# A hybrid encoder trunk on one core: a fourth PSUM tile for the attention heads, a shorter schedule for the modulation chunks, and priority for two last features instead of one

## The chip, the cores and the metric

The kernel runs on one core of one Trainium2 chip. Its time is the device time of one execution in microseconds (us). Three executions were timed before the change, and one more was profiled. TensorE (PE) does the matmuls, with its weight loads shown apart as PEld; VectorE (DVE), ScalarE (ACT) and GpSimd (POOL) work on vectors; SyncE (SP) issues the transfers.

## The reference

Two layers work on one sequence of 256 tokens with 2048 features, in float32:

```python
mod = c_act @ ada_w[l] + ada_b[l]                       # 6 x 2048 values: shift, scale, gate, twice
h = rmsnorm(x, norm_mix[l]) * (1.0 + sc_a) + sh_a
qa, ka, va, qb, kb, vb, ga, gb = split_cols(h @ w_in[l])
ya = window_attention(qa, ka, va, sink_a[l]) @ w_proj_a[l]      # 8 heads, 2 key heads, rotary
yb = neighbourhood_attention(qb, kb, vb, rel_bias_b[l]) @ w_proj_b[l]   # 8 heads
merged = jax.nn.sigmoid(ga) * ya + jax.nn.sigmoid(gb) * yb
x = x + gt_a * (merged @ w_out[l])
h = rmsnorm(x, norm_ffn[l]) * (1.0 + sc_m) + sh_m
u = depthwise_conv(h @ w_up[l], conv_w[l], conv_b[l])
g, v = jnp.split(u, 2, axis=-1)
x = x + gt_m * ((jax.nn.silu(g) * v) @ w_down[l])
```

rmsnorm divides by the root of the mean square of x, so each of the two norms of a layer needs the sum of the squares of all 2048 features, and the next product can be scaled only when the last feature of x is there.

## The kernel before

**Weights.** All matrices are streamed in the order of their use, 1 MB at a time: a unit is 16 blocks of 128x128. A unit is loaded into one of four `raw` buffers (L319). It is then halved into two parts `hl` of eight blocks: ACT casts the high part (L327) and DVE subtracts it from the original for the low part (L328). There are four `hl` buffers, so two units are held at a time. For a block PE multiplies the high weights with the high activations, and adds the two mixed products: three matmuls for most matrices (L374 to L376 with features of x in columns, L448 to L450 with tokens), and two for w_up and w_down where activations lie side by side (L370, L371). A name such as `hl_98_0` is the first half of unit 98, and `ps_98_16` the PSUM tile whose product begins behind unit 98's last block before it.

**Order of a layer.** Units 0 to 99 are w_in, w_proj_a, w_proj_b and w_out, units 100 to 231 w_up and w_down in three groups. During w_in of layer 0 the attention heads run on the side, one step of each live head per unit. A head's steps take PSUM tiles from the pool `ax`: `qtp` for the turned queries and keys (L681, evicted by ACT into packA or packB at L682), `sc` for the scores (L710), `tp` for the turned probabilities (L742), `po` for the result (L750). The projections themselves accumulate in the pool `mm` of four tiles.

**Squares' sums.** As each feature block `mo` of x (0 to 15) gets its residual (L1122), ACT squares it (L499) and DVE adds the square to `sqa` (L501); of the last block the square is kept apart. A matmul with a column of 1/2048 then sums `sqa` over the partitions (L508, `first`), and another the last square (`squares`). The tile for that (`ssm` behind w_out, `ssf` behind w_down) has a PSUM bank of its own, with a tag `ss`. The scaled features for the next product (`bare`, L596 and L597) are made at the same time, without the root, which is applied to the products later.

**Modulation.** The product for `mod` is done on DVE, in 192 chunks of 1 MB in each of which one column of 128 values is made (L227 loads, L230 multiplies and sums; all but three are loaded into the `raw` buffers too). The tables `ADA_PLAN_0` and `ADA_PLAN_1` say how many chunks are to be done when a unit of a layer is reached, with straight lines between the corners. The end of layer 0 needs 96 chunks for its own gates, and layer 1's first norm 32 of the next 96.

**Scheduler.** The tile framework puts the instructions of each engine into an order by their priority and readiness, so a short edit moves many instructions. In the code `urgent(...)` gives a block a higher priority than what comes before it in the program: the last features of w_out (both layers) and of the last w_down group are marked so, from `mo >= ENDING` on, and their units are fetched ahead (`prefetch`).

In w_out the features 13, 14 and 15 begin in the tiles ps_97_16, ps_98_16 and ps_99_16, each with 48 matmuls. In the last w_down group features 13, 14 and 15 are ps_230_9, ps_231_6 and ps_232_3, each with 26 matmuls.

Of the kernel before, what the change touches and what calls it, by code (L numbers as in the profile page):

```python
# [9 lines left out]
F32 = mybir.dt.float32  # L10
# [46 lines left out]
FIRST_TURN = 3  # L57
OUT_TURNS = [range(0, FIRST_TURN)] + [[mo] for mo in range(FIRST_TURN, KC)]

ADA_PLAN_0 = [(38, 32), (58, 48), (76, 66), (84, 70), (98, 80), (108, 80), (231, 132)]  # L60
ADA_PLAN_1 = [(8, 132), (76, 164), (84, 168), (99, 176), (108, 176), (128, 184), (142, 192)]

HASTE = range(76, 108)
FIRST_PLAN = [(0, 6), (10, 17), (42, 48)]

LEAD = 52
ENDING = 15

WARM_IN = [8, 4, 6]
WARM_ROW = 16  # L70
# [76 lines left out]
def encoder(ctx: ExitStack, tc: tile.TileContext, a: dict, out: bass.AP):  # L147
# [8 lines left out]
    at = pool("at", 2)  # L156
    sm = pool("sm", 3)
    mm = pool("mm", 4, space=bass.MemoryType.PSUM)
    ax = pool("ax", 3, space=bass.MemoryType.PSUM)

    ident = const.tile([P, P], F32, name="ident")
    make_identity(nc, ident[:])
# [327 lines left out]
    class Squares:  # L490


        def __init__(self, name):
            self.acc = ev.tile([P, S], F32, name="sqa", tag="sqa", bufs=1)
            self.ps = ax.tile([P, 2, 2], F32, name=name, tag="ss", bufs=1)

        def add(self, mo):
            sq = self.acc if mo == 0 else ev.tile([P, S], F32, name="sq", tag="z")
# [10 lines left out]
                )  # L509

        def first(self):
            self.total(0, self.acc)
            self.head = sm.tile([P, 2], F32, name="nsa", tag="nsa")
            nc.vector.tensor_scalar(out=self.head[:], in0=self.ps[:, 0], scalar1=EPS, scalar2=None, op0=ALU.add)

    def rsqrt(dst, src, n, k):

# [48 lines left out]
    class Bare:  # L566
# [36 lines left out]
        def squares(self):  # L603
            self.sums.total(1, self.sums.last)
            ss = sm.tile([P, 2], F32, name="nss", tag="nss")
            nc.vector.tensor_tensor(out=ss[:], in0=self.sums.head[:], in1=self.sums.ps[:, 1], op=ALU.add)  # L606
            self.rs = roots(ss)

        def roots(self):
# [199 lines left out]
    with tc.high_priority():  # L809
        one = place("b0", 12, F32, "one")[:1, 0, :P]  # L810
        nc.vector.memset(one, 1.0)
        cbs = []
        for i in range(0, D, 512):
            cbs.append(mm.tile([P, 512], F32, name="cb", tag="mm"))
            nc.tensor.matmul(cbs[-1][:], one, cact[:1, i : i + 512], start=True, stop=True)

        def activated(i):
            tc.keep_in_program_order(
                nc.scalar.activation(out=cact[:, 512 * i : 512 * (i + 1)], in_=cbs[i][:], func=AF.Silu)
            )  # L820

        sqs = []
        for i in range(KC // 4):
            sq = place(("y0", "y1", "y2", "a")[i], 12 if i == 3 else 4, F32, f"sq_in{i}")
            xs = x[:, 4 * i : 4 * i + 4]
            if i == 1:
                nc.vector.tensor_tensor(out=sq[:, :4], in0=xs, in1=xs, op=ALU.mult)
                activated(0)
                activated(1)
            else:  # L830
                tc.keep_in_program_order(nc.scalar.activation(out=sq[:, :4], in_=xs, func=AF.Square))
            sqs.append(sq)
        activated(2)
        activated(3)
        acc = sqs[0]
        for sq in sqs[1:]:
            nc.vector.tensor_tensor(out=acc[:], in0=acc[:], in1=sq[:, :4], op=ALU.add)
        nc.vector.tensor_tensor(out=acc[:, :2], in0=acc[:, :2], in1=acc[:, 2:4], op=ALU.add)
        warm(WARM_IN[0])
        ps = ax.tile([P, 2], F32, name="ss_in", tag="ss", bufs=1)  # L840
        for t in range(2):
            for i in range(2):
                tc.keep_in_program_order(
                    nc.tensor.matmul(
                        ps[:, t : t + 1], acc[:, i, t * P : (t + 1) * P], mean[:], start=i == 0, stop=i == 1
                    )
                )
        warm(WARM_IN[1])
        nc.scalar.activation(out=mean_sq[:], in_=ps[:], func=AF.Identity, bias=eps[:])

    tables = []

# [457 lines left out]
```

## Time and profile before

| | us |
|---|---|
| three executions | 2565.88, 2569.01, 2570.2 |
| median | 2569.01 |
| profiled execution | 2565.51 |
| its span on the core | 2563.7 |
| PE busy, DVE busy, ACT busy | 2538.5, 2205.4, 1451.8 |

A row of a timeline gives start, duration, engine, line, operation and tiles; brackets hold the idle time just before and the instruction that ended it. PE's matmuls are pipelined, so durations overlap; what counts is the distance between starts. The duration of a 256-column matmul is shown as 0.28 us, while starts are 0.11 us apart.

### The profile page before, as it was taken

The numbers are of one execution on the slowest core, as the hardware profiler recorded it, in microseconds if no ns is written. First come the engines' busy times: TensorE is split into PE (matmuls) and PEld (weight loads), VectorE is DVE, ScalarE is ACT, GpSimd is POOL, SyncE is SP. The second block draws the span as 40 slices with busy tenths as digits, with TensorE's granted clock in tenths as the row PEclk, the third lists the DMA queues.
The fourth block names the chain that finished last, engine by engine and source line by source line (L and its number), as shares of the span: only waits on it lengthen the run. The fifth ranks groups of instructions, "written<-read, shape, count | busy, mean of one in ns | idle before, by whom it ended". The sixth has DMA issues, their size and how long they took to land.

```text
span 2563.7 us, 39982 instructions
## 1 busy us (share of the span) xinstructions
PE 2538.5 (99%) x15636; PEld 2322.9 (91%) x15636; DVE 2205.4 (86%) x3159; ACT 1451.8 (57%) x2388; POOL 256.6 (10%) x329
## 2 busy tenths in 40 slices
PE   8999999999999999999999999999999999999999
PEld 7888888899999999999998888999999999999998
DVE  8999998998998899799987788979889987766775
ACT  5445865456664565456565676554576546654663
POOL 0000100000000000000004678720000000000000
PEclk9999999999999999999999999999999999999999
DMA  9998789886788778777767676777848875555554
GB/s 373 354 348 309 256 320 362 330 317 224 262 293 303 261 281 302 287 280 283 275 228 279 263 278 263 299 295 295 294 167 295 297 288 203 197 199 203 205 198 148
DMA packets 102143, 699.75 MB, mean 273 GB/s; under 512 B 12865, under 2 KB 15169, under 8 KB 18113
## 3 DMA queue, kind: packets, MB, share of 16 engines
q1 hardware_dynamic: 101954, 697.20, 73.4%
q8 instruction: 122, 2.00, 0.3%
q14 instruction: 67, 0.55, 0.1%
HBM read 695.06 MB, written 2.10 MB: 272 GB/s over the span
## 4 chain that ended last, share of the span: by engine, by line
PE 72%; DVE 15%; DMA 4%; issue 3%; ACT 3%; POOL 2%; SPq 0%; DVEq 0%; ACTq 0%; POOLq 0%
PE ps L370 31%; PE ps L371 16%; DVE hl L328 6%; PE ps_t L449 5%; PE ps_t L450 5%; PE ps_t L448 5%; DVE aw L230 4%; DMA aw<-in_aw 4%; PE ps L376 3%; PE ps L374 3%; PE ps L375 2%; ACT hl L327 1%; POOL packA L302 1%; DVE x L1122 1%; DMA w<-in_ws 1%
## 5 line engine op out<-in xcount | busy, mean ns | idle before, releaser
L328 DVE TENSOR_TENSOR hl<-w,hl 128x1024 fp32r<-128x1024 f32 x928 | 1131.0, 1227 | 232.0 <-ACT hl L327 229.4
L327 ACT CAST hl<-w 128x1024 fp32r<-128x1024 f32 x928 | 966.1, 1049 | 597.6 <-PE ps L371 263.0
L370 PE MATMUL ps<-h,hl 128*128 128x512 f32 x2432 | 796.8, 382 | 0.0
L371 PE MATMUL ps<-h,hl 128*128 128x256 f32 x2432 | 662.9, 273 | 0.0
L370 PEld LDWEIGHTS ps<-h,hl 128*128 128x128 f32 x2432 | 459.7, 189 | 63.9
L371 PEld LDWEIGHTS ps<-h,hl 128*128 128x128 f32 x2432 | 466.9, 192 | 0.0
L230 DVE CUSTOM_DVE_ANT_0 aw<-aw,cact,ab 128x2048 f32<-128x2048 f32 x189 | 444.5, 2353 | 9.9 <-DMA aw<-in_aw 9.8
L449 PE MATMUL ps_t<-hl,h 128*128 128x512 f32 x960 | 366.2, 382 | 4.1 <-DVE hl L328 3.8
L448 PE MATMUL ps_t<-hl,h 128*128 128x512 f32 x960 | 363.1, 383 | 3.8 <-ACT h L555 2.0
L450 PE MATMUL ps_t<-hl,h 128*128 128x512 f32 x960 | 364.7, 380 | 0.0
L449 PEld LDWEIGHTS ps_t<-hl,h 128*128 128x128 f32 x960 | 181.9, 190 | 34.1 <-DVE hl L328 9.1
L448 PEld LDWEIGHTS ps_t<-hl,h 128*128 128x128 f32 x960 | 181.1, 189 | 31.2 <-ACT hl L327 4.1
L450 PEld LDWEIGHTS ps_t<-hl,h 128*128 128x128 f32 x960 | 181.8, 189 | 25.7 <-DVE h L556 0.2
L370 PE MATMUL ps<-act_o,hl 128*128 128x512 f32 x512 | 170.5, 382 | 0.0
L1149 DVE SCALAR_TENSOR_TENSOR u<-both,cw,u 128x255 f32<-128x255 f32 x304 | 146.2, 481 | 3.8
L376 PE MATMUL ps<-merged,hl 128*128 128x256 f32 x512 | 140.9, 275 | 0.9 <-DVE hl L328 0.9
L374 PE MATMUL ps<-merged,hl 128*128 128x256 f32 x512 | 140.9, 276 | 0.4 <-DVE gb L481 0.4
L375 PE MATMUL ps<-merged,hl 128*128 128x256 f32 x512 | 140.7, 275 | 0.0
L371 PE MATMUL ps<-act_o,hl 128*128 128x256 f32 x512 | 139.6, 273 | 0.0
L1171 ACT COPY both<-ps 128x256 f32<-128x256 f32 x152 | 56.4, 371 | 124.6 <-PE ps L371 123.5
L1122 DVE SCALAR_TENSOR_TENSOR x<-ps,mod,x 128x256 f32<-128x256 f32 x224 | 105.6, 482 | 21.5 <-PE ps L371 19.4
L535 POOL TENSOR_TENSOR nrs<-nss,mhalf 128x2 f32<-128x2 f32 x3 | 2.1, 697 | 1173.6 <-DVE nss L606 1173.6
(264 smaller groups left out, 4336.4 us busy)
## 6 DMA issues: line engine op xcount, KB each, us to landing
w<-in_ws SPq DMA_DIRECT2D x463, 1024.0 KB, 4.8
aw<-in_aw SPq DMA_DIRECT2D x189, 1024.0 KB, 5.0
p<-in_bias SPq DMA_DIRECT2D x16, 256.0 KB, 3.6
x<-in_xT SPq DMA_DIRECT2D x4, 512.0 KB, 5.6
aw_o<-in_aw SPq DMA_DIRECT2D x2, 1024.0 KB, 12.4
out<-x SPq DMA_DIRECT2D x16, 128.0 KB, 1.8
w<-in_ws SPq DMA_DIRECT2D x2, 512.0 KB, 11.6
aw_b<-in_aw SPq DMA_DIRECT2D x1, 1024.0 KB, 16.8
```

The costliest lines, as they stand in the source:

```text
L230: product = nc.vector.tensor_tensor_reduce(out=raw[:], in0=raw[:], in1=cact[:], scale=1.0, scalar=ab[:, i : i + 1], op0=ALU.mult, op1=ALU. ...
L327: nc.scalar.copy(hl[:, 0], r)
L328: nc.vector.tensor_tensor(out=hl[:, 1], in0=r, in1=hl[:, 0].bitcast(F32), op=ALU.subtract)
L370: nc.tensor.matmul(ps[:], hi, act.both, start=first, stop=False)
L371: nc.tensor.matmul(ps[:, :S], lo, act.high, start=False, stop=last)
L374: nc.tensor.matmul(out, hi, act[0], start=first, stop=False)
L375: nc.tensor.matmul(ps[:, :S], hi, act[1], start=False, stop=False)
L376: nc.tensor.matmul(out, lo, act[0], start=False, stop=last)
L448: nc.tensor.matmul(ps[:], xh, hi, start=kc == kcs[0], stop=False)
L449: nc.tensor.matmul(ps[:], xh, lo, start=False, stop=False)
L450: nc.tensor.matmul(ps[:], xl, hi, start=False, stop=kc == kcs[-1])
L1149: nc.vector.scalar_tensor_tensor(out=u[:, to], in0=ps[:, of], scalar=w[:, j : j + 1], in1=u[:, to], op0=ALU.mult, op1=ALU.add)
```

## The change

It has three parts.

1. The pool `ax` has four PSUM tiles instead of three. The bank for it comes from the squares' sums, which no longer have one of their own: `first` takes a tile of `ax` when the sum is made, and `ss_in`, the same sum for the input, does so too.
2. The last corner of `ADA_PLAN_0` is at unit 216 instead of 231. The 52 chunks that were spread over units 108 to 231 now lie between 108 and 216, and there is none in the last 15 units of layer 0.
3. `ENDING` is 14 instead of 15. Features 14 and 15 have the priority, not feature 15 alone, in w_out of both layers and in the last w_down group of both layers.

```diff
-ADA_PLAN_0 = [(38, 32), (58, 48), (76, 66), (84, 70), (98, 80), (108, 80), (231, 132)]
+ADA_PLAN_0 = [(38, 32), (58, 48), (76, 66), (84, 70), (98, 80), (108, 80), (216, 132)]
...
-ENDING = 15
+ENDING = 14
...
-    ax = pool("ax", 3, space=bass.MemoryType.PSUM)
+    ax = pool("ax", 4, space=bass.MemoryType.PSUM)
...
         def __init__(self, name):
             self.acc = ev.tile([P, S], F32, name="sqa", tag="sqa", bufs=1)
-            self.ps = ax.tile([P, 2, 2], F32, name=name, tag="ss", bufs=1)
+            self.name = name
...
         def first(self):
+            self.ps = ax.tile([P, 2, S], F32, name=self.name, tag="ax")
             self.total(0, self.acc)
             self.head = sm.tile([P, 2], F32, name="nsa", tag="nsa")
-            nc.vector.tensor_scalar(out=self.head[:], in0=self.ps[:, 0], scalar1=EPS, scalar2=None, op0=ALU.add)
+            nc.vector.tensor_scalar(out=self.head[:], in0=self.ps[:, 0, :2], scalar1=EPS, scalar2=None, op0=ALU.add)
...
-            nc.vector.tensor_tensor(out=ss[:], in0=self.sums.head[:], in1=self.sums.ps[:, 1], op=ALU.add)
+            nc.vector.tensor_tensor(out=ss[:], in0=self.sums.head[:], in1=self.sums.ps[:, 1, :2], op=ALU.add)
...
-        ps = ax.tile([P, 2], F32, name="ss_in", tag="ss", bufs=1)
+        ps = ax.tile([P, 512], F32, name="ss_in", tag="ax")
...
-        nc.scalar.activation(out=mean_sq[:], in_=ps[:], func=AF.Identity, bias=eps[:])
+        nc.scalar.activation(out=mean_sq[:], in_=ps[:, :2], func=AF.Identity, bias=eps[:])
```

From line 512 on, the lines of the changed kernel have numbers that are higher by one.

The order on PE at the heads of layer 0, where unit 46 begins (a piece of the difference; - is before, + the change):

```order
-L681 MATMUL qtp<-ident,qn 128x128 x8
-L742 MATMUL tp<-ident,p 128x128 x4
+L682 MATMUL qtp<-ident,qn 128x128 x8
+L743 MATMUL tp<-ident,p 128x128 x4
+L711 MATMUL sc<-packA_209 128x256 x2
 L448 MATMUL ps_46_t_2200<-hl_46_0_2166,h_0_157 128x512
 L449 MATMUL ps_46_t_2200<-hl_46_0_2166,h_0_157 128x512
 L450 MATMUL ps_46_t_2200<-hl_46_0_2166,h_0_157 128x512
 L448 MATMUL ps_46_t_2201<-hl_46_0_2166,h_0_157 128x512
-L710 MATMUL sc<-packA_209 128x256 x2
```

The scores are put four matmuls earlier; around units 47 to 52 sc and tp move ahead by three to nine rows in the same way.

The order on PE in w_out of layer 0, before, where feature 13 (ps_97_16) ends:

```order
L375 MATMUL ps_97_16_0_5229<-merged_3993,hl_97_1_5235 128x256
L376 MATMUL ps_97_16_0_5229<-merged_3993,hl_97_1_5235 128x256
L374 MATMUL ps_98_16_0_5298<-merged_3993,hl_98_0_5301 128x256
L374 MATMUL ps_99_16_0_5379<-merged_3993,hl_99_0_5365 128x256
L375 MATMUL ps_99_16_0_5379<-merged_3993,hl_99_0_5365 128x256
L376 MATMUL ps_99_16_0_5379<-merged_3993,hl_99_0_5365 128x256
```

And in the change, where feature 12 (ps_96_16) ends:

```order
L376 MATMUL ps_96_16_0_5160<-merged_3993,hl_96_1_5166 128x256
L374 MATMUL ps_97_16_0_5228<-merged_3993,hl_97_0_5231 128x256
L374 MATMUL ps_98_16_0_5297<-merged_3993,hl_98_0_5300 128x256
L375 MATMUL ps_98_16_0_5297<-merged_3993,hl_98_0_5300 128x256
L376 MATMUL ps_98_16_0_5297<-merged_3993,hl_98_0_5300 128x256
L374 MATMUL ps_98_16_0_5297<-merged_3993,hl_98_0_5300 128x256
```

Before, feature 13 is finished first, and 14 stops after one matmul to let 15 pass. Now 13 stops after one matmul, 14 and 15 are done, and 13 comes last.

The order on DVE at the end of layer 0, before, from the residual of the feature that ends last (ps_231_6, feature 14) to the reading of its sum:

```order
L1122 SCALAR_TENSOR_TENSOR x<-ps_231_6_0_12205,mod_158,x 128x256
L328 TENSOR_TENSOR hl_1_0_12262<-w_1_12260,hl_1_0_12262 128x1024
L1122 SCALAR_TENSOR_TENSOR x<-ps_231_6_0_12205,mod_158,x 128x256
L328 TENSOR_TENSOR hl_1_1_12265<-w_1_12260,hl_1_1_12265 128x1024
L501 TENSOR_TENSOR sqa<-sqa,sq 128x256
L597 SCALAR_TENSOR_TENSOR bare_0_b_11589<-x,amod_8113,bare_0_b_11589 128x256
L514 TENSOR_SCALAR nsa<-ssf_11586 128x2
```

And in the change, where it is feature 13 (ps_230_9):

```order
L1123 SCALAR_TENSOR_TENSOR x<-ps_230_9_0_12163,mod_158,x 128x256
L602 TENSOR_TENSOR bare_0_qn<-mod_7859,bare_0_qn 128x1
L328 TENSOR_TENSOR hl_1_1_12264<-w_1_12259,hl_1_1_12264 128x1024
L1123 SCALAR_TENSOR_TENSOR x<-ps_230_9_0_12163,mod_158,x 128x256
L501 TENSOR_TENSOR sqa<-sqa,sq 128x256 x2
L598 SCALAR_TENSOR_TENSOR bare_0_b_11607<-x,amod_7864,bare_0_b_11607 128x256
L515 TENSOR_SCALAR nsa<-ssf_12288 128x2
```

One split instead of two stands between the residual's start and the sum, and two additions follow each other. On PE the first matmul of ssf comes 40 matmuls after the last one of w_down, where it came 31 after it.

## The prediction

> **What bounds the kernel now.** I read the page first, then who waited for whom on TensorE, then the stretches around each wait, then the order of time there. Two rows of the page, and the rows of PE's waits that belong to the places of the change (total us, times, longest):
>
> ```profile
> PE 2538.5 (99%) x15636; PEld 2322.9 (91%) x15636; DVE 2205.4 (86%) x3159; ACT 1451.8 (57%) x2388; POOL 256.6 (10%) x329
> L328 DVE TENSOR_TENSOR hl<-w,hl 128x1024 fp32r<-128x1024 f32 x928 | 1131.0, 1227 | 232.0 <-ACT hl L327 229.4
> ...
> PE ps_t L449 <- DVE hl L328: 3.8, 10, 0.6
> PE ps L376 <- DVE hl L328: 3.4, 5, 1.5
> PE sc L710 <- ACT packB L682: 2.4, 1, 2.4
> PE ssf L508 <- DVE sqa L501: 1.5, 1, 1.5
> PE tp L742 <- ACT packB L682: 0.7, 2, 0.4
> ```
>
> TensorE is busy for 99% of the 2563.7 us, so the change can win only where it waits, or where its clock is lowered. Of the waits above, sc and tp (3.1 us) are for a PSUM tile of the heads, ssf (1.5 us) is for the sum of squares, and the rest is for weights: `hl` is the halved weight that ACT casts (L327) and DVE completes (L328). Behind the two longest waits the granted clock falls. The columns are the stretch, its length, busy us of PE, PEld, DVE, ACT and POOL, the granted clock and the DMA:
>
> ```profile
> 276.00:279.00 3.00, 1.00 (x6) 0.54 (x4) 3.00 (x5) 2.97 (x13) 0.00 (x0) 1.00 0.82 309
> 279.00:283.00 4.00, 3.56 (x9) 2.90 (x10) 3.84 (x10) 3.63 (x13) 0.00 (x0) 0.57 0.56 188
> 283.00:292.00 9.00, 9.00 (x51) 7.83 (x51) 8.02 (x18) 7.91 (x29) 1.64 (x1) 1.00 0.79 292
> 292.00:331.00 39.00, 38.26 (x215) 33.89 (x213) 38.39 (x89) 35.09 (x95) 5.24 (x2) 1.00 0.59 210
> 331.00:386.00 55.00, 55.00 (x275) 48.67 (x274) 54.97 (x83) 31.73 (x59) 0.00 (x0) 1.00 0.90 340
> 386.00:440.00 54.00, 54.00 (x267) 47.72 (x266) 47.63 (x64) 29.04 (x47) 0.00 (x0) 1.00 0.97 362
> ...
> 1306.00:1311.00 5.00, 5.00 (x32) 5.00 (x32) 1.46 (x3) 0.84 (x2) 0.70 (x1) 0.66 0.67 231
> ...
> 1628.00:1636.00 8.00, 6.49 (x58) 6.30 (x57) 8.00 (x12) 3.96 (x6) 5.64 (x7) 1.00 0.73 265
> ```
>
> So one lowered spell costs 4 us x (1 - 0.57) = 1.7 us, and 5 us x (1 - 0.66) = 1.7 us the other time. It followed a wait of 2.4 us and one of 1.5 us; the 1.5 us wait for weights around 1630 (the longest of L376) was not followed by one.
>
> **The heads of layer 0 (fourth tile).** What can be removed on TensorE is 2.4 (sc) + 1.7 (spell) + 0.7 (tp) = 4.8 us. With four tiles sc and tp no longer stand behind the eviction of qtp (packB, L682), so I take these waits as gone. But how much reaches the end is decided by the weights. DVE has no room: from 276 to 331 us it is idle for 55 - (3.00 + 3.84 + 8.02 + 38.39) = 1.75 us, from 331 to 386 for 0.03 us, and its order there is almost the same in the changed kernel. The halves just ahead of that, as DVE finishes and as PE takes them:
>
> ```profile
> 328.14 1.22 DVE L328 TENSOR_TENSOR hl<-w,hl 128x1024 fp32r<-128x1024 f32 x1
> 331.37 0.38 PE L449 MATMUL ps_t<-hl,oA 128*128 128x512 f32 x1
> ...
> 336.03 2.35 DVE L328 TENSOR_TENSOR hl<-w,hl 128x1024 fp32r<-128x1024 f32 x2
> 337.43 0.38 PE L449 MATMUL ps_t<-hl,oA 128*128 128x512 f32 x1
> ```
>
> The first is ready at 329.36 and used 2.0 us later; the first of the two at 336.03 is ready at about 337.25 and used 0.18 us later. A TensorE that is 4.8 us early waits there for all but 0.2 us of it, unless DVE is early too. DVE can be early by no more than its idle 1.75 us. More than half of that is one wait in the heads' own chain, behind sc and the exponentials:
>
> ```profile
> 286.45 0.16 DVE L726 TENSOR_TENSOR den<-den,es 128x2 f32<-128x2 f32 x1 [0.98 <-ACT es L725]
> ```
>
> That one goes, and a part of the rest: I take 1.2 us as won. After 386 us the transfers run at 0.97, and PE waits for weights again around 454 to 474 us (the row of 440 to 480 us):
>
> ```profile
> PE ps_t L449 <- DVE hl L328: 1.3, 3, 0.6
> ```
>
> There everything is tied to transfers, which start earlier by what DVE is early. **-1.2 us**; bounds 0 (DVE wins nothing) and -4.8 (all is kept).
>
> **Priority for feature 14, w_out of layer 0.** The two last features are now both ahead of feature 13, so unit 98's weights are asked for 48 matmuls earlier, before feature 13's own:
>
> ```profile
> 586.95 0.28 PE L374 MATMUL ps<-merged,hl 128*128 128x256 f32 x1
> 592.20 0.28 PE L376 MATMUL ps<-merged,hl 128*128 128x256 f32 x1
> 592.97 0.38 PE L376 MATMUL ps<-merged,hl 128*128 128x256 f32 x1 [0.16 <-DVE hl L328]
> 603.46 0.28 PE L374 MATMUL ps<-bare_a,hl 128*128 128x258 f32 x1
> ...
> 587.16 1.98 ACT L327 CAST hl<-w 128x1024 fp32r<-128x1024 f32 x2
> 588.25 1.23 DVE L328 TENSOR_TENSOR hl<-w,hl 128x1024 fp32r<-128x1024 f32 x1
> ```
>
> The first two rows are 47 matmuls apart, 0.1115 us each. At 586.95 PE starts feature 13 with one matmul and then wants unit 98 at 587.07. Its first half is cast by 588.20 (the two casts at 587.16 overlap; the first takes 1.03) and completed by DVE at 589.48. The high half costs 588.20 - 587.07 = 1.1 us of waiting, two matmuls follow, and the low half costs 589.48 - 588.46 = 1.0 us. Then both halves of unit 97 stay held, so both halves of unit 99 go through the one buffer that unit 98's first half frees at about 592.0; cast 1.03 and split 1.22 make it ready at 594.3 against a use at 594.2, and the second is as tight: 0.2 us together. Before, the same 144 matmuls took 603.46 - 586.95 = 16.51 us for 144 x 0.1115 = 16.06, so 0.45 is given back. 1.1 + 1.0 + 0.2 - 0.45 = **+2.0 us** (rounded up by the hand-over of some 0.04 us at each wait); bounds 0, if the scheduler's order lets the splits come earlier, and +3.7, with a spell of lowered clock behind it. The two waits have matmuls between them and neither reaches 1.5 us, so I count no spell.
>
> **The same in layer 1.**
>
> ```profile
> 1845.46 0.28 PE L374 MATMUL ps<-merged,hl 128*128 128x256 f32 x1
> 1862.86 0.28 PE L374 MATMUL ps<-bare_a,hl 128*128 128x258 f32 x1
> ...
> 1843.49 2.35 DVE L230 CUSTOM_DVE_ANT_0 aw<-aw,cact,ab 128x2048 f32<-128x2048 f32 x1 [0.96 <-DMA aw<-in_aw]
> 1846.50 2.36 DVE L328 TENSOR_TENSOR hl<-w,hl 128x1024 fp32r<-128x1024 f32 x2
> ```
>
> Here a modulation chunk (L230, 2.35 us) stands on DVE ahead of the split of unit 98's first half, the second of the two at 1846.50, which ends at 1848.86. After one matmul on unit 97, the two high ones on unit 98 and three more, PE is at 1846.13: a wait of 2.75 us; later 0.2 as above. Before, 17.40 us for 16.06 of matmuls: 1.35 given back. 2.75 + 0.2 - 1.35 = +1.6. This wait is longer than both that were followed by a spell, so I add one: 1.6 + 1.7 = **+3.3 us**; bounds 0 and +4.3, if the chunk, which itself waited 0.96 us for its transfer, lands 1 us later.
>
> [...]
>
> **w_down at the end of layer 0 (no chunks, priority).**
>
> ```profile
> 1287.54 0.38 PE L370 MATMUL ps<-act_o,hl 128*128 128x512 f32 x1
> 1303.83 0.28 PE L374 MATMUL ps<-bare_a,hl 128*128 128x258 f32 x1
> 1305.64 0.61 PE L508 MATMUL ssf<-mean,sqa 128*128 128x1 f32 x4 [1.53 <-DVE sqa L501]
> ...
> 1284.25 2.37 DVE L230 CUSTOM_DVE_ANT_0 aw<-aw,cact,ab 128x2048 f32<-128x2048 f32 x1
> 1288.45 1.24 DVE L328 TENSOR_TENSOR hl<-w,hl 128x1024 fp32r<-128x1024 f32 x1
> 1303.64 0.48 DVE L1122 SCALAR_TENSOR_TENSOR x<-ps,mod,x 128x256 f32<-128x256 f32 x1
> 1305.16 0.42 DVE L501 TENSOR_TENSOR sqa<-sqa,sq 128x256 f32<-128x256 f32 x1
> ```
>
> ssf costs 1305.64 - 1303.94 = 1.7 us, the spell 1.7, some 0.1 besides: 3.5 us. Now ssf has 40 matmuls ahead of it since the last group's end instead of 31 (0.1115 each: 1.0 us later), and feature 14's square is added long before; only 13's residual (L1122, twice, with one split between), square and two additions follow the last matmul: about 0.5 + 1.2 + 0.5 + 0.4 + 0.7 = 3.3 us plus a wait for the cast of 0.6, against 4.5 us of matmuls. So ssf does not wait. Against it: unit 231's first half is now wanted 13 matmuls after 1287.54 (0.164 us each, a long and a short one being 0.33), at 1289.7. DVE, without the chunk of 1284.25, comes to its end after three splits (1.13 us from start to start), four residuals and a modulated copy (0.39 each) and an addition (0.34): 5.7 us, at 1290.0. With the cast and small hand-overs I take 0.7 us of waits. -3.5 + 0.8 = **-2.7 us** (0.1 for what else comes late); bounds -3.5 and 0.
>
> **The chunks' new place.** Seven chunks more between units 108 and 216, 7 x 2.35 = 16.5 us of DVE:
>
> ```profile
> 650.00:1210.00 560.00, 560.00 (x3484) 516.67 (x3483) 502.67 (x711) 316.06 (x470) 0.00 (x0) 1.00 0.77 285
> ```
>
> DVE goes from 502.67 to 519 of 560 us (93%), PE does not wait there in this row, and the transfers are at 0.77. **0**; bounds 0 and +1.5, where a half comes late by part of one chunk. If the cover went, it would cost at most those 16.5 us.
>
> **The kernel's end.** The last group's features end in the other order; after the last matmul the same two residuals remain:
>
> ```profile
> 2559.92 1.00 DVE L1122 SCALAR_TENSOR_TENSOR x<-ps,mod,x 128x256 f32<-128x256 f32 x2 [3.04 <-PE ps L371]
> ```
>
> A wait for unit 231's weights as at the end of layer 0, less hidden work: **+0.3 us** (0 to +0.5). Layer 1's heads hardly change their order, and their waits there are for hl: 0. The squares' sums in the other pool take a tile for three instructions at the seams, when no head runs: 0.
>
> **Sum.** -1.2 + 2.0 + 3.3 - 2.7 + 0 + 0.3 = +1.7 us. The profiled execution took 2565.51 us; the median is 3.5 above it, so on the median's basis I say 2569.0 + 1.7 = **2570.7 us**: no change, since 0.2% (5.1 us) is about what a measurement of this kernel can tell.
>
> **Rivals.** (A) The weights follow: the first splits after the heads come early enough, or transfers do, and the 4.8 us stay; the earlier splits of units 98 and 231 hide the new waits. -4.8 - 2.7 = -7.5: 2561.5. For it: 2.0 us of slack at 331. Against: 0.18 us at 337 and a full DVE. (B) Slower: the waits for unit 98 take the place of those removed, and lowered clock follows all of them, at w_out in both layers and at w_down, where the wait for unit 231 grows past 1.5 us and eats the gain. -1.2 + 3.7 + 3.3 + 0 + 0.3 = +6.1: 2575.1. It decides from 1.5 us of waiting in one piece; for it speaks 1306, against it 1630. (C) No spell follows in either layer, as around 1630: +1.7 - 1.7 = 0.0: 2569.0. [...] (D) The fourth tile does not help, because sc waits for packB's data and not for the tile: then -1.2 goes, and 2572. Against it: sc reads packA, and packB is only what frees the tile.
>
> **Chances.** Forecast 0.38, C 0.17, D 0.08, A 0.14, B 0.23. A is the faster case, with 0.02 from C's lower edge: 0.16. B is the slower one: 0.23. Same: 0.61. The forecast's own range is 2567 to 2573; to hold 8 in 10 it reaches to A's upper part and past B: 2563 to 2576.5.
>
> **What would show it.** Right: no sc or tp among PE's waits, clock 1.00 from 276 to 283; new waits of ps_t for hl between 331 and 345 us and longer ones at 454 to 474; ps L374 or L376 waiting about 2 us near 588 and 2.8 near 1846; no wait of ssf, clock 1.00 from 1303 to 1312; DVE's busy share up from 650 to 1210. Wrong: PE passing 345 us more than 2 us earlier than before (then A), lowered clock at 588 or 1295 (then B), or a PE wait of over 1 us between 650 and 1210.

## The result and the profile after

| | before | after |
|---|---|---|
| median of 9 executions, us | 2568.71 | 2574.11 |
| lowest and highest, us | 2564.28, 2570.39 | 2571.7, 2580.4 |
| span of the profiled execution, us | 2563.7 | 2571.9 |
| ratio, with 95% interval | | 1.0037 [1.0027, 1.0047] |

The changed kernel is slower: by 5.4 us between the medians, 8.2 between the two profiled executions, and some 9.5 by the ratio, whose interval goes from 7 to 12 us. The forecast was 2570.7 us and no change. The time lies inside the wide range that was given (2563 to 2576.5) but above the forecast's own (2567 to 2573), and the direction was not the likeliest one: the slower case had a chance of 0.23.

On the page of the changed kernel, TensorE's row:

```profile
PE 2541.8 (99%) x15636; PEld 2324.1 (90%) x15636; DVE 2203.0 (86%) x3159; ACT 1448.5 (56%) x2388; POOL 259.4 (10%) x329
```

Its waits (total us, times, longest), those that belong to the places of the change:

```profile
PE ps L376 <- DVE hl L328: 4.5, 6, 1.5
...
PE po L751 <- ACT pT L465: 2.2, 1, 2.2
PE ps L371 <- DVE hl L328: 2.2, 5, 1.0
PE ps L374 <- ACT hl L327: 2.1, 3, 1.7
PE ssf L508 <- DVE sqa L501: 0.5, 1, 0.5
...
PE sc L711 <- ACT packB L683: 0.3, 1, 0.3
```

The waits for sc (2.4), tp (0.7) and most of the wait for ssf (1.5) are gone, as intended by the edits. New are `po`, a wait of 2.2 us in the heads; L371, five waits in w_up, where before there was none; and in the row of L374 one of 1.7 us for the first half of unit 98 in w_out (before, that row had 0.4 us in all). The stretches around them, with the columns as in the prediction (length, busy us of PE, PEld, DVE, ACT and POOL, granted clock, DMA):

```profile
285.00:290.00 5.00, 2.80 (x17) 2.27 (x16) 5.00 (x15) 4.88 (x19) 1.64 (x1) 0.96 0.92 375
290.00:293.00 3.00, 3.00 (x10) 2.46 (x9) 2.63 (x8) 2.76 (x12) 1.51 (x1) 0.50 0.37 93
...
587.00:592.00 5.00, 2.55 (x12) 2.25 (x12) 5.00 (x9) 3.48 (x6) 0.00 (x0) 0.80 0.99 375
592.00:597.00 5.00, 4.94 (x36) 4.68 (x36) 1.55 (x3) 1.14 (x2) 0.00 (x0) 0.86 0.81 284
...
1178.00:1228.00 50.00, 48.07 (x289) 43.22 (x288) 43.46 (x63) 28.84 (x46) 0.00 (x0) 1.00 0.74 274
...
1300.00:1320.00 20.00, 19.36 (x145) 18.23 (x145) 13.26 (x21) 10.10 (x15) 0.69 (x1) 1.00 0.48 158
```

To see where time goes for good, the same matmul of PE is looked up in two traces: the first one on a given unit. The table gives how much later (or, with a minus, earlier) it starts than in the kernel before. A step between two columns is what that stretch costs. It is worked out from the starts of PE's matmuls, one profiled execution of each kernel; e1 to e12 are the kernels of the experiments below. At 269 us alone the starts lie between 0.3 us earlier and 3.1 later, with the same edits or not, so steps count and not levels. One piece of the scatter has a size. Where the granted clock falls, it is at 0.50 for 3.4 us (before: 279.2 to 282.6 and 1306.6 to 1310.0 us; changed kernel: 289.6 to 293.0), in e5 from 1854 us on for twice that, which costs 1.7 us (or 3.4). The profiled execution of the kernel before has two such spells inside the table, from 279 and from 1307 us, so a kernel that does not have them steps by -1.7 there with no merit of its own.

| us before | 269 | 297 | 471 | 576 | 610 | 1096 | 1232 | 1316 | 1731 | 1840 | 1875 | 2539 |
|---|---|---|---|---|---|---|---|---|---|---|---|---|
| layer, unit | 0, 45 | 0, 48 | 0, 76 | 0, 95 | 0, 101 | 0, 193 | 0, 219 | 1, 2 | 1, 76 | 1, 96 | 1, 102 | 1, 228 |
| after | 0.2 | 0.5 | -0.7 | -0.1 | 5.0 | 5.0 | 8.6 | 6.5 | 6.3 | 6.9 | 7.7 | 7.7 |
| e1 | 1.7 | 2.0 | 1.5 | 3.1 | 3.3 | 3.3 | 3.3 | 1.6 | 1.5 | 2.5 | 2.4 | 2.4 |
| e2 | 1.8 | 0.4 | 0.5 | 1.2 | 1.4 | 1.4 | 4.8 | 1.5 | 1.8 | 2.5 | 1.2 | 1.2 |
| e3 | 1.8 | 0.4 | -1.0 | 1.0 | 5.7 | 5.7 | 5.7 | 4.6 | 4.9 | 10.4 | 15.4 | 15.4 |
| e4 | -0.3 | -1.7 | -2.7 | -2.8 | -3.2 | -3.2 | 0.2 | -3.1 | -3.4 | -3.2 | -1.9 | -1.9 |
| e5 | 2.3 | 2.8 | 2.1 | 2.4 | 5.5 | 5.4 | 8.9 | 5.6 | 5.5 | 5.6 | 11.2 | 11.2 |
| e6 | 1.7 | 2.5 | 2.3 | 2.3 | 1.9 | 1.9 | 5.9 | 3.7 | 3.5 | 4.6 | 4.0 | 4.0 |
| e7 | 3.1 | 3.4 | 2.2 | 2.1 | 2.3 | 2.3 | 2.3 | -1.0 | -1.3 | 1.9 | 1.9 | 1.8 |
| e8 | -0.1 | -1.4 | -2.6 | -2.6 | -3.0 | -1.8 | -1.8 | -5.1 | -5.4 | -4.4 | -5.6 | -5.6 |
| e9 | 1.9 | 2.0 | 7.8 | 21.6 | 21.2 | 21.2 | 21.2 | 19.5 | 19.7 | 20.4 | 20.2 | 20.2 |
| e10 | 1.5 | 1.7 | 10.0 | 25.3 | 25.9 | 25.9 | 25.9 | 24.6 | 24.4 | 28.7 | 33.1 | 33.1 |
| e11 | 1.7 | 2.1 | 1.3 | 1.3 | 0.9 | 0.9 | 0.9 | -2.4 | -2.6 | -1.3 | 1.4 | 1.4 |
| e12 | 1.6 | -0.7 | -0.8 | -0.5 | 0.1 | 0.1 | 0.1 | -1.5 | 1.5 | 2.7 | 3.2 | 3.2 |

For the changed kernel: two places cost, w_out of layer 0 (576 to 610 us: +5.1) and the chunks' new place (1096 to 1232: +3.7); the end of layer 0 steps by -2.2 and the heads, taken from 269 to 471, by -0.9. How much of these two the change has earned is a question for the experiments. The rest is small: 0.6 ahead of w_out, 1.4 around w_out of layer 1, and 0.5 behind the last column.

### The profile page after: what moved, and what is told of

Same layout as the page of the kernel before. It is cut to its first block, busy times and chain, and to the rows that moved or that the text cites. A ratio compares the mean times of both kernels' runs of the same rounds, so it can differ in the third digit from the quotient of the medians.

```text
span 2571.9 us, 39995 instructions
## 1 busy us (share of the span) xinstructions
PE 2541.8 (99%) x15636; PEld 2324.1 (90%) x15636; DVE 2203.0 (86%) x3159; ACT 1448.5 (56%) x2388; POOL 259.4 (10%) x329
## 4 chain that ended last, share of the span: by engine, by line
PE 72%; DVE 15%; ACT 4%; DMA 4%; issue 3%; POOL 2%; SPq 0%; ACTq 0%; DVEq 0%; POOLq 0%
PE ps L370 30%; PE ps L371 15%; DVE hl L328 6%; PE ps_t L449 5%; PE ps_t L450 5%; PE ps_t L448 5%; PE ps L376 4%; PE ps L374 4%; DVE aw L230 4%; PE ps L375 4%; ACT hl L327 2%; DMA aw<-in_aw 2%; DMA w<-in_ws 1%; POOL p L302 1%; POOL packA L302 1%
## 5 line engine op out<-in xcount | busy, mean ns | idle before, releaser
L371 PE MATMUL ps<-h,hl 128*128 128x256 f32 x2432 | 663.8, 273 | 2.2 <-DVE hl L328 2.2
L371 PEld LDWEIGHTS ps<-h,hl 128*128 128x128 f32 x2432 | 467.4, 192 | 3.9 <-DVE hl L328 3.9
L1150 DVE SCALAR_TENSOR_TENSOR u<-both,cw,u 128x255 f32<-128x255 f32 x304 | 146.0, 480 | 3.3
L374 PE MATMUL ps<-merged,hl 128*128 128x256 f32 x512 | 142.1, 278 | 2.1 <-ACT hl L327 1.7
L371 PE MATMUL ps<-act_o,hl 128*128 128x256 f32 x512 | 139.3, 273 | 0.0
L1123 DVE SCALAR_TENSOR_TENSOR x<-ps,mod,x 128x256 f32<-128x256 f32 x224 | 105.0, 480 | 36.0 <-PE ps L371 25.9
```

The costliest lines, as they stand in the source:

```text
L371: nc.tensor.matmul(ps[:, :S], lo, act.high, start=False, stop=last)
L374: nc.tensor.matmul(out, hi, act[0], start=first, stop=False)
L1150: nc.vector.scalar_tensor_tensor(out=u[:, to], in0=ps[:, of], scalar=w[:, j : j + 1], in1=u[:, to], op0=ALU.mult, op1=ALU.add)
```

## The experiments

The change has three parts, so the first three kernels do one each.

**e1, the fourth tile alone.**

```diff
 (the changed kernel with)
-(108, 80), (216, 132)]
+(108, 80), (231, 132)]
-ENDING = 14
+ENDING = 15
```

> Only the fourth tile (the squares' sums in the same pool); plan and priority as before. Theory M (read from the two traces): the wait of sc is gone, but one of about 2.2 us for ACT's pT takes its place some 7 us later, followed by a spell of lowered clock as before; what stays by 470 us is -1, and the whole is -1.1 to 0 us. Theory F (as forecast): -1.2 us, with the new waits being for hl between 331 and 345 us. If the heads' waits were worth what they show, -4.8 us.

Measured: 2566.16 us against 2567.54, ratio 0.9996 [0.9985, 1.0006]. From 269 to 471 us it wins 0.2 of the 4.8 us that stood on PE. The steps from 269 to 297 us show why. With the fourth tile they are +0.3 to +0.8 where a lowered clock follows the wait for po (after, e1, e5, e6, e7, e11) and -1.4 and -1.3 where none does (e4, e8). Without it they are 0 to +0.2 where a lowered clock follows the wait for sc (before, e9, e10) and -1.4 where none does (e2, e3). So the tile moved the wait to the next step of the heads and took nothing off it; what differs is the spell. From 269 to 471 us the kernels without the tile step by -1.3 (e2) and -2.8 (e3), so no gain of the tile can be told from the scatter there either.

**e2, the plan alone.**

```diff
 (the kernel before with)
-(108, 80), (231, 132)]
+(108, 80), (216, 132)]
```

> Only the plan: no chunk in the last 15 units of layer 0. Theory M: about +3 us from waits of PE for hl in units 209 to 217 (1180 to 1230 us), one each second unit, and the wait of ssf near 1304 stays within 0.5 us of its 1.7, since it hangs on the last feature and not on the chunks: +2 to +3.5. Theory F: 0 (DVE has room), -0.5 to +1.5.

Measured: 2566.87, ratio 0.9996 [0.9987, 1.0005]. Two steps cancel in the table: +3.4 from 1096 to 1232 us and -3.2 from 1232 to 1316. So the plan alone takes away the wait for ssf, which the prediction had credited to plan and priority together, and pays for it earlier; each of the two expectations had missed one of the steps. Half of the 3.2 us is not the plan's. e1, e9 and e12 have the old plan and the old order, and they wait for ssf for 1.5 us as the kernel before does, but their steps are -1.6 and -1.7, the cost of one spell that the kernel before has there and they, by these steps, do not. The lowered clock at 1307 belongs to that one execution of the kernel before. Against these three kernels the plan is worth some 1.6 us here, and it costs 3.4 in w_up.

**e3, the priority alone.**

```diff
 (the kernel before with)
-ENDING = 15
+ENDING = 14
```

> Only the priority for feature 14. Theory M: +5 us at w_out of layer 0 (about 1.8 and 1.0 us of waits near 587 us and a spell of lowered clock), +1 in layer 1, and at the end of w_down of layer 0 between -2.3 us (the order alone does it) and 0 (the chunks there spoil it): +3.5 to +6. Theory F: +2.0, +3.3, -2.7 and +0.3: +2.9.

Measured: 2574.77, ratio 1.0031 [1.002, 1.0041]. This part is slower alone: +4.7 at w_out of layer 0, and +5.0 at w_out of layer 1 (1840 to 1875; 5.5 more came from 1731 to 1840, where e7 without the priority also loses 3.3). At the end of layer 0 its step is -1.1, smaller than that of e1, e9 and e12, which have neither plan nor priority: there the priority alone costs half a microsecond.

**e4, tile and plan, without the priority.**

```diff
 (the changed kernel with)
-ENDING = 14
+ENDING = 15
```

> The fourth tile and the plan, priority as before: the sum of the first two if they do not touch each other. Theory M: +1 to +3.5. Theory F: -1.2. If the parts are separate, this and the third kernel add up to the whole change (+5.4 us).

Measured: 2567.25, ratio 1.0000 [0.9987, 1.0012]: what makes the changed kernel slower is the priority. The step of +3.4 at the chunks' new place stays, and so does the one of -3.3 at the end of layer 0. The time lies between the two expectations.

**e5 and e6, the priority in one of its two places**, with tile and plan as in e4.

```diff
 (e5: the changed kernel, 14 in w_out, 15 in w_down)
-                ending = last and mos[0] >= ENDING
+                ending = last and mos[0] >= ENDING + 1
 (e6: 15 in w_out, 14 in w_down)
-            with urgent(mos[0] >= ENDING):
+            with urgent(mos[0] >= ENDING + 1):
```

> The whole change, but with the old priority in w_down: only w_out has feature 14 before 13. Theory M: the cost of the change lies here, +6 us in layer 0 (waits for unit 98's halves and a lowered clock behind them) and 0.5 to 4 in layer 1: +5.5 to +8. Theory F: 2.0 + 3.3 with -1.2 and, for w_down without the new order, up to -2.7 from the plan: +1.4 to +4.

> The whole change, but with the old priority in w_out: only the last w_down group has feature 14 before 13. Theory M: ssf's wait was the chunks' work and not the order's, so the new order there only costs: +1 over the fourth kernel of the first set (2567.25 us, that is 0 against before): 0 to +2. Theory F: the order itself takes 3.5 us away at 1304 and costs 0.8: -3.5 to -1.

Measured: e5 2576.01, ratio 1.0032 [1.002, 1.0044]; e6 2569.1, ratio 1.0005 [0.9996, 1.0013]. The loss sits in w_out. In w_down the priority wins nothing on top of the plan: with it the end of layer 0 steps by -2.2 (e6, after), without it by -3.3 (e4, e5), and the kernel's end loses 0.5 us in the four kernels that have it (after, e3, e6, e10).

**What w_out waits for.** The timeline of the changed kernel around unit 98 (start, duration; in brackets the idle time just before and what ended it), first PE, then DVE, then ACT:

```profile
586.84 0.28 PE L374 MATMUL ps<-merged,hl 128*128 128x256 f32 x1
588.77 0.38 PE L374 MATMUL ps<-merged,hl 128*128 128x256 f32 x1 [1.66 <-ACT hl L327]
588.98 0.28 PE L375 MATMUL ps<-merged,hl 128*128 128x256 f32 x1
590.05 0.58 PE L376 MATMUL ps<-merged,hl 128*128 128x256 f32 x1 [0.80 <-DVE hl L328]
...
583.04 2.35 DVE L230 CUSTOM_DVE_ANT_0 aw<-aw,cact,ab 128x2048 f32<-128x2048 f32 x1 [0.40 <-DMA aw<-in_aw]
...
585.31 1.22 DVE L328 TENSOR_TENSOR hl<-w,hl 128x1024 fp32r<-128x1024 f32 x1
586.45 0.48 DVE L1123 SCALAR_TENSOR_TENSOR x<-ps,mod,x 128x256 f32<-128x256 f32 x1
...
586.96 0.42 ACT L499 ACTIVATE sq<-x 128x256 f32<-128x256 f32 x1 [3.45 <-DVE x L1123]
587.29 0.49 ACT L597 ACTIVATE bare_b<-x,amod 128x256 fp32r<-128x256 f32 x1
587.69 1.98 ACT L327 CAST hl<-w 128x1024 fp32r<-128x1024 f32 x2
```

PE stands 588.77 - 586.84 - 0.11 = 1.82 us for the high half and 590.05 - 588.98 - 0.11 = 0.96 for the low half. The cast of unit 98 is not late because ACT is busy: ACT sits idle for 3.45 us with the square of an earlier feature at the head of its order. That square needs a residual of DVE (L1123), and the residual stands on DVE behind a split and a modulation chunk, which itself waited 0.40 us for its transfer. In before's order the same chain exists, but PE has another unit's 48 matmuls to do meanwhile. In e3 and e5 the chunk did not wait for its transfer, and the first wait is 1.2 us instead of 1.7.

**e9 and e10, no chunk beside w_out**, as a pair: e9 with the old priority as the control, e10 with the new one. All ten chunks of units 84 to 98 are brought forward to units 58 to 84.

```diff
 (e9: the kernel before with; e10: the same and ENDING = 14)
-(58, 48), (76, 66), (84, 70), (98, 80), (108, 80), (231, 132)]
+(58, 48), (76, 70), (84, 80), (108, 80), (231, 132)]
```

> Control for the next one: the kernel before with its chunks 48 to 79 all placed in units 58 to 84, so that none lies beside w_out of layer 0 (there are five from unit 91 on before). No theory needs it faster or slower; the stretch before 480 us, where transfers are the bound, may lose some: -1 to +3 against before.

> The same with feature 14's priority in w_out and w_down. Theory Q (unit 98's halves are late at 588 us because the cast stands behind a square that stands behind a residual that stands behind a chunk on DVE, and because a chunk's transfer is ahead of the unit's): without the chunks the waits near 588 us in layer 0 fall from 2.8 us to under 1 and no lowered clock follows; the cost of the priority in layer 0 is 0.5 to 1.5 us over the control, and with layer 1 (unchanged, +4) 4.5 to 6. Theory R (asking for a unit 48 matmuls early costs that much by itself, whatever stands beside it): the waits stay at 2 to 3 us, and the whole is 7 to 9 over the control.

Measured: e9 2589.7, ratio 1.0085 [1.0073, 1.0098]; e10 2593.38, ratio 1.0111 [1.0097, 1.0125]. The control missed its expectation by some 20 us, nearly all of it between 402 and 528 us on the scale of the kernel before (units 64 to 86), where ten more megabytes had to come:

```profile
440.00:480.00 40.00, 35.96 (x162) 29.71 (x160) 35.81 (x39) 15.85 (x21) 0.00 (x0) 1.00 0.98 392
```

The transfers stand at 0.98 of their share and 392 GB/s; ten megabytes at that rate are 10 / 0.392 = 25 us. So this stage is bound by transfers, and chunks must not move there. The pair still answers its question. In w_out of layer 0 neither kernel waits for unit 98's halves, and the step from 576 to 610 us is -0.4 in the control and +0.6 in e10: without a chunk on DVE the priority costs 1.0 us there, where it costs 3.1 (e5, with no lowered clock) to 5.1 (the changed kernel, with one) beside chunks. The pair takes away the chunk's work and its transfer together; that the work on DVE is the larger part is read from the timeline above. In layer 1, where the chunks were left as they were, e10 loses as e3 does (4.5 us from 1840 to 1875).

**w_out of layer 1.** The changed kernel itself loses only 0.8 us there, e5 loses 5.6, with the same order of instructions on DVE there. e5's timeline and stretch:

```profile
1855.30 0.58 PE L376 MATMUL ps<-merged,hl 128*128 128x256 f32 x1 [3.39 <-DVE hl L328]
...
1849.81 2.35 DVE L230 CUSTOM_DVE_ANT_0 aw<-aw,cact,ab 128x2048 f32<-128x2048 f32 x1 [0.88 <-DMA aw<-in_aw]
...
1852.89 2.35 DVE L328 TENSOR_TENSOR hl<-w,hl 128x1024 fp32r<-128x1024 f32 x2
```

```profile
1855.00:1860.00 5.00, 4.71 (x22) 4.71 (x23) 2.66 (x6) 1.01 (x3) 0.00 (x0) 0.50 1.01 416
```

And the changed kernel's timeline there:

```profile
1854.14 0.38 PE L376 MATMUL ps<-merged,hl 128*128 128x256 f32 x1 [0.93 <-DVE hl L328]
...
1848.65 2.35 DVE L230 CUSTOM_DVE_ANT_0 aw<-aw,cact,ab 128x2048 f32<-128x2048 f32 x1 [0.95 <-DMA aw<-in_aw]
...
1851.73 2.35 DVE L328 TENSOR_TENSOR hl<-w,hl 128x1024 fp32r<-128x1024 f32 x2
```

The chunk waits for its transfer in both, and the splits of unit 98 follow behind it. In e5 the transfer lands 1.2 us later (1849.81 against 1848.65) and PE comes 1.3 us earlier (unit 96 starts at 1840.1 + 5.6 against 1840.1 + 6.9), so the wait is 3.39 us instead of 0.93, and the clock is halved for 5 us behind it. The kernels without the priority vary in this stage too: PE's losses between 1840 and 1890 us, from the distances of its starts, are 1.5 to 5.4 us and 3.0 on the mean in nine of them (before, e1, e2, e4, e6, e7, e8, e11, e12), against 3.2, 7.5 and 8.0 in those with it (after, e3, e5).

**e7 and e8, why the chunks' new place costs 3.7 us.** The prediction had a mean busy share of 93% there and PE without a wait. Two theories were set against each other: DVE has too little room, or the chunks fall on a bad place of a repeating pattern. e7 stretches the plan a little, which changes the spacing; e8 keeps the spacing and shifts the line by one unit.

```diff
 (e7: tile and plan, as e4, with)
-(108, 80), (216, 132)]
+(108, 80), (227, 132)]
 (e8: as e4, with)
-(108, 80), (216, 132)]
+(109, 80), (217, 132)]
```

> Fourth tile, old priority, and the plan's last corner at unit 227: one chunk in 2.29 units instead of 2.08, and none in the last 4 units. Theory P (what costs is a chunk at the same place of every second unit): no waits between 1180 and 1230 us, and ssf's wait and the lowered clock at 1304 still mostly gone: -2 to -4. If ssf needs all 15 units free: -1 to 0.

> Fourth tile, old priority, and the plan's line moved by one unit (109 to 217 instead of 108 to 216): as many chunks, as dense, but in group 3 of w_up beside the other half of each pair of features (units 195, 197 ... 217). Theory P (the place decides: beside the second feature of a pair, where DVE also has the product and the split of the activation, each chunk takes 0.7 us of slack): the 3.4 us of waits at 1184 to 1230 us are gone, and less than 1 us appears near unit 163: -2 to -3.5 against before. Theory A (the amount of chunks per time decides): the waits stay, 3 us or more: 0 to +1.

Measured: e7 2564.56, ratio 0.9989 [0.9981, 0.9998]; e8 2563.61, ratio 0.9991 [0.9983, 1.0]. Both have no step from 1096 to 1232 us and keep the step at the end of layer 0 (-3.3 each). The stretch of the five waits, in the kernel before and then in e8:

```profile
1178.00:1228.00 50.00, 50.00 (x307) 46.02 (x307) 46.95 (x73) 31.04 (x51) 0.00 (x0) 1.00 0.78 291
1178.00:1228.00 50.00, 50.00 (x307) 45.97 (x306) 48.10 (x71) 32.41 (x49) 0.00 (x0) 1.00 0.82 308
```

Room was not the matter: in e8 DVE is busy for 48.10 of 50 us (96%) and PE never waits; in the changed kernel DVE is busy for 43.46 (87%) and PE waits. (The page's five waits add up to 2.2 us; by the distances between PE's starts each costs some 0.3 us more, and the stretch 3.7.) What the pattern is shows in the timelines. The changed kernel, DVE and then ACT, one round of a pair of features in w_up:

```profile
1169.10 1.22 DVE L328 TENSOR_TENSOR hl<-w,hl 128x1024 fp32r<-128x1024 f32 x1 [1.14 <-ACT hl L327]
1170.24 0.48 DVE L1150 SCALAR_TENSOR_TENSOR u<-both,cw,u 128x255 f32<-128x255 f32 x1
1170.64 2.35 DVE L230 CUSTOM_DVE_ANT_0 aw<-aw,cact,ab 128x2048 f32<-128x2048 f32 x1
...
1178.11 0.48 DVE L1150 SCALAR_TENSOR_TENSOR u<-both,cw,u 128x255 f32<-128x255 f32 x1
...
1180.07 1.23 DVE L328 TENSOR_TENSOR hl<-w,hl 128x1024 fp32r<-128x1024 f32 x1 [1.15 <-ACT hl L327]
1181.21 0.48 DVE L1150 SCALAR_TENSOR_TENSOR u<-both,cw,u 128x255 f32<-128x255 f32 x1
1181.61 2.35 DVE L230 CUSTOM_DVE_ANT_0 aw<-aw,cact,ab 128x2048 f32<-128x2048 f32 x1
...
1178.68 0.42 ACT L1184 ACTIVATE u<-u 128x256 f32<-128x256 f32 x1 [1.65 <-DVE u L1150]
1179.00 1.04 ACT L327 CAST hl<-w 128x1024 fp32r<-128x1024 f32 x1
```

And e8:

```profile
1175.86 2.35 DVE L230 CUSTOM_DVE_ANT_0 aw<-aw,cact,ab 128x2048 f32<-128x2048 f32 x1
...
1186.35 2.35 DVE L230 CUSTOM_DVE_ANT_0 aw<-aw,cact,ab 128x2048 f32<-128x2048 f32 x1
...
1178.20 0.37 ACT L1172 COPY both<-ps 128x256 f32<-128x256 f32 x1 [1.53 <-PE ps L371]
1178.71 0.42 ACT L1184 ACTIVATE u<-u 128x256 f32<-128x256 f32 x1
```

In the changed kernel a ring closes between DVE and ACT: the convolution's last step on DVE (L1150 at 1178.11) lets ACT's activation start (L1184, 1.65 us idle before it), ACT's cast comes behind it in order, DVE's next split waits 1.15 us for that cast, and then come the chunk and all else up to the next L1150. PE is not in this ring: no idle time of DVE or ACT in this round ended on PE. One round takes 1180.07 - 1169.10 = 10.97 us. PE needs 10.49 us for the same two units: in e8 PE sets the pace (ACT waits for PE's ps, 1.53), and the chunks there are 1186.35 - 1175.86 = 10.49 apart. So with every pair DVE falls back by half a microsecond or more. How long the first half of each unit is ready before PE uses it (us, worked out from both ends; * marks a unit with a chunk beside it) shows it:

```
unit     196   197   198   199   200   201   202   203   204   205   206   207
before   5.5*  3.7   4.8*  3.6   5.2   4.6*  3.7   4.8*  3.6   4.8*  3.7   4.8
after    5.5*  3.7   5.2*  2.9   4.5*  2.1   3.6*  1.5   3.1*  0.9   2.0*  0.1
e8       3.7   4.8*  3.6   4.9*  3.7   4.9*  3.6   4.8*  3.7   4.8*  3.6   4.8*
```

A unit of w_up is one feature, and two features make a pair. With 108 / 52 = 2.08 units from chunk to chunk, against 123 / 52 = 2.37 before, the chunk comes back beside the same feature of the pair for a dozen pairs. Beside the one nothing is lost; beside the other the reserve of 5.5 us is eaten at some 0.7 us a pair, and from then on PE waits once in every pair.

**e11, both phases right.** By this theory e8 must lose a little in an earlier group of w_up, where its shift puts chunks beside the wrong feature; the table has +1.2 between 610 and 1096 us. e11 chooses the corners so that both groups have them beside the right one.

```diff
 (as e4, with)
-(108, 80), (216, 132)]
+(108, 80), (166, 108), (182, 115), (217, 132)]
```

> Fourth tile, old priority, and a plan with corners at 166, 182 and 217 whose chunks lie beside the first feature of each pair in both groups of w_up (units 140 to 166 even, 195 to 217 odd), none in the last 14 units. Theory P: no waits for hl between 650 and 1290 us, and none of ssf: 1.2 us better than the shifted plan: -3 to -4.5 against before. If the place is not what counts: 0 to -2.5.

Measured: 2564.79, ratio 0.9992 [0.9983, 1.0001]. In the table there is no step at all from 610 to 1232 us, and -3.3 at the end of layer 0, as the theory has it. The time is no better than that of e7 and e8, and the expected -3 to -4.5 us was missed (some -2 by the ratio); its profiled execution lost 2.7 us in w_out of layer 1, where the kernels scatter.

**e12, the heads without mixer B's squares.** In the heads the wait for sc became a wait for po. The changed kernel's timeline there, PE, ACT and DVE:

```profile
285.94 0.38 PE L450 MATMUL ps_t<-hl,h 128*128 128x512 f32 x1
288.51 0.49 PE L751 MATMUL po<-pT,vA 128*128 128x256 f32 x2 [2.20 <-ACT pT L465]
...
286.23 0.91 ACT L731 ACTIVATE p<-p,ri 128x256 f32<-128x256 f32 x2
...
287.89 0.57 ACT L465 CAST pT<-tp 128x512 fp32r<-128x512 f32 x1
...
282.94 2.34 DVE L230 CUSTOM_DVE_ANT_0 aw<-aw,cact,ab 128x2048 f32<-128x2048 f32 x1
...
285.98 0.15 DVE L729 RECIPROCAL ri<-den 128x2 f32<-128x2 f32 x1
```

The turned probabilities pT are cast by ACT at 287.89. Ahead of them ACT works almost without a gap (4.88 of the 5.00 us from 285 to 290): among others the scaling by `ri` at 286.23 and, behind that, four instructions for mixer B's squares (L636). DVE makes `ri` at 285.98 behind a chunk of 2.34 us, but it is there when ACT comes to it. e12 takes the squares away: it leaves out the squares of mixer B's queries and keys, so its heads B are not normalized.

```diff
 (as e1, with, in qk_rows)
+        if rot is None:
+            nc.gpsimd.memset(ss[:], 128.0)
-        for t, ps in enumerate(pss):
+        for t, ps in enumerate(pss if rot is not None else ()):
```

> Fourth tile with old plan and priority, and ACT relieved in the heads: the squares of mixer B's queries and keys (64 activations of about 0.5 us from start to start, between 250 and 350 us) are left out in both layers, with a constant in place of their sums, so the heads of mixer B are not normalised. Theory H (the heads' waits come from ACT's queue, and what they cost is not passed on, since DVE has no room until 386 us and transfers none until 474): the waits of sc and po between 276 and 296 us go or shrink to under 1 us, new waits for hl appear between 330 and 475 us, and the whole is -1 to -3 against before. Theory W (the heads' waits are worth what they show): -4.5 to -6.

Measured: 2567.75, ratio 1.0007 [0.9998, 1.0016]. Both expectations were missed. A wait for po of 3.0 us still stands in the heads. From 269 to 471 us the kernel wins 2.4, but its step up to 297 us is -2.3, so no lowered clock is in it, and e3, without the fourth tile, wins 2.8. With the squares gone it is ACT that waits for DVE ahead of pT (0.96 and 0.65 us for `ri`), and DVE is busy without a gap from 276 to 288 us, with a chunk in it. So ACT's squares alone do not hold pT up; whether DVE's chunk does was not tested, since no experiment moved it. Between 1316 and 1731 us the kernel loses 3.0 us.

## Why the prediction was wrong, step by step

The measured steps are against the one profiled execution of the kernel before, with its two spells of lowered clock.

| step | forecast, us | measured in the changed kernel | in the experiments |
|---|---|---|---|
| heads of layer 0 | -1.2 | -0.9 | e1 -0.2, e4 -2.4, e6 +0.6; without the tile e2 -1.3, e3 -2.8 |
| w_out of layer 0 | +2.0 | +5.1 | e3 +4.7, e5 +3.1, e10 +0.6 |
| chunks' new place | 0 | +3.7 | e2 +3.4, e4 +3.4, e7 0, e8 0 (and +1.2 in an earlier group), e11 0 |
| end of layer 0 | -2.7 | -2.2 | e2 -3.2, e4 -3.3, e3 -1.1; neither plan nor priority: e1, e9 -1.7, e12 -1.6 |
| w_out of layer 1 | +3.3 | +0.8 | e3 +5.0, e5 +5.6, e10 +4.5 |
| the kernel's end | +0.3 | +0.5 | e3, e6, e10 +0.5 |

The sum of the terms was +1.7 us, the measured steps add up to +7.0. Two terms failed: the chunks' new place (3.7 us more than forecast) and w_out of layer 0 (3.1 more). w_out of layer 1 took 2.5 us back in this execution. That the change is slower comes from the second: e4, with the chunks' new place and without the priority, stands at 1.0000.

**The term that failed in its mechanism is "The chunks' new place: 0".** It rested on one mean over 560 us (DVE at 93%, PE without a wait) and on the bound of one late chunk, 1.5 us. The mechanism, a ring of DVE and ACT that is longer than PE's round when the chunk stands beside the wrong feature of a pair, was not thought of; the busy share would not have shown it, as e8's 96% without a wait against 87% with waits tells. The last sentence of the prediction named "a PE wait of over 1 us between 650 and 1210" as a sign of error; the three waits up to 1210 us are of 0.4 at most, and the longest of the five, 1.0, comes at 1219. It might have been read ahead: the order of the changed kernel has the chunks' places, and the trace has the rows of a round.

**w_out of layer 0 was right in its mechanism and too small.** The waits came as forecast, 1.82 and 0.96 us against 1.1 and 1.0. Two things are missing. The cast was taken from before's trace, at 587.16, as if nothing stood ahead of it; it stands behind a chunk, by way of the residual and the square, and the chunk's 0.40 us of waiting for its transfer moves all of it. And no lowered clock was counted because neither wait reaches 1.5 us; the first did, and with 0.80 and 0.86 in the two stretches behind it 5 x 0.2 + 5 x 0.14 = 1.7 us at most are due to that. In e3 the first wait is only 1.2 us and a lowered clock follows all the same. In e5, with the same two waits, the clock stays at 1.00, and the stage costs 3.1.

**The gain at the end of layer 0 had the right size by luck, and the wrong author.** Of the 3.5 us that the prediction had ssf cost, 1.7 were the lowered clock, which the kernel before had in this one execution and which e1, e9 and e12, by their steps, do not have behind the same wait of 1.5 us. Against these three, the plan wins some 1.6 us and the changed kernel some 0.5. The prediction put the ssf wait's end down to the new order of features 13 and 14. e2 shows that taking the chunks away is enough, and e4 against after shows that the order takes back 1.1 us, near the 0.8 that were counted for unit 231.

**w_out of layer 1** happened by the mechanism that was worked out in e3, e5 and e10 (one wait of 3.0 to 3.5 us instead of 2.75, and a lowered clock with it). It cost 4.5 to 5.6 us there, more than the bound of 4.3. In the profiled execution of the changed kernel it hardly happened. The size hangs on when one transfer lands, which the prediction had as a bound.

**The heads** came out near the forecast by luck. The waits for sc and tp went, but the time did not run on to the weights at 331 us: PE stood at once, for 2.20 us, in the next step of the heads, and up to 297 us the kernels with and without the tile step alike when their clock is alike. So nothing was won that DVE's missing room could have taken back, and that argument was not put to the test.

**The rivals.** B, the slower one, came nearest in its time: it had unit 98's wait with a lowered clock behind it at w_out of layer 0. It did not have the chunks, and at the end of layer 0 the step that it wrote off came, so its nearness in time is in part luck. A fell: the heads' 4.8 us did not stay, as e1 shows (0.9996, and 0.2 us by 471 us), and the waits at w_out were not hidden. C, no lowered clock behind the new waits, fell at 588 us. D fell: sc waits 0.3 us with four tiles instead of 2.4.

Whether a version beats both kernels: e7 and e8 have the point estimates for it, 0.9989 and 0.9991 against the kernel before, some 2.5 us (e11 0.9992); the interval of e7 ends at 0.9998, so this is at the edge of what can be told. Both are the tile and a plan without chunks in the last units, at a place where the chunks fall on the right feature, and the old priority.

## What to carry to other kernels

An engine's mean busy share said nothing here on a task that comes back at the same place of a repeating pattern (DVE at 96% without a wait of PE in e8, at 87% with waits in the changed kernel): compare the length of the ring that it lengthens with the round of the engine that sets the pace, and choose the spacing so that it does not come back beside the same step. When a reorder makes a unit wanted earlier, price it from what stands ahead of its producers in their own orders, transfers included, and not from when they happened to run before. A wait that is taken away can come back at the next step of its own chain, as sc's 2.4 us came back as 2.20 for po, so look there before you count it as won. And a spell of lowered clock in one execution is not yet a cost of the kernel: look for it in a second execution, and price it with a chance.

## What the runs showed of the hardware

In these runs the clock does not follow from the length of a wait alone. The spells that can be read in short stretches are 0.50 for 3.4 us, in e5 from 1854 us on twice that (0.94, 0.50 and 0.90 in 1848 to 1855, 1855 to 1860 and 1860 to 1865 us). Whether one follows a wait differs between the profiled executions, one of each kernel:

| wait of PE, us | kernels that have it | followed by a lowered clock in | granted clock behind it |
|---|---|---|---|
| po, 2.20 | after, e1, e4 to e8, e11 | all but e4 and e8 | 290 to 293 us: after 0.50, e1 0.64, e5 0.64, e6 0.80, e7 0.88, e11 0.66; e4 and e8 1.00 |
| po, 3.0 | e12 | none | by its step of -2.3 from 269 to 297 us |
| sc, 2.4 | before, e2, e3, e9, e10 | before, e9, e10 | 280 to 284 us: before 0.67, e9 0.73, e10 0.62; e2 and e3 1.00 |
| ssf, 1.5 | before, e1, e9, e12 | before | 1306 to 1311 us: before 0.66; the others by their steps of -1.6 and -1.7 |
| unit 98 in layer 0, 1.2 to 1.7 and 0.8 | after, e3, e5 | after, e3 | 592 to 597 us: after 0.86, e3 0.75; e5 1.00 |
| unit 98 in layer 1, 3.0 to 3.5 | e3, e5, e10 | all three | e3 0.66 (1860 to 1865 us), e5 0.50 (1855 to 1860), e10 0.82 (1880 to 1885) |

e2 behind the wait for sc (the kernel before has 0.67 in this stretch), and e8 in the same stretch as the changed kernel's second row above (clock 0.50):

```profile
280.00:284.00 4.00, 2.80 (x13) 2.49 (x14) 4.00 (x9) 3.94 (x14) 0.00 (x0) 1.00 0.55 184
...
290.00:293.00 3.00, 3.00 (x15) 2.65 (x14) 2.72 (x11) 3.00 (x12) 1.64 (x1) 1.00 0.43 126
```

So a spell of some 1.7 us should have been priced with a chance, and not by a limit on the wait. A wait of 2.20 us was followed by one in six of eight kernels; what decides it, no run here shows.
